# Differential attention: one score tile per map, the turns' bank given up, and low weights times high values only

## The chip, the cores and the metric

The kernel runs on one core of a Trainium2 chip. The metric is the device time of one execution in microseconds; the time of a kernel is the median of its runs. A profiled execution has a time of its own, its span, from the first instruction to the last.

## What is computed

The reference runs two trunk layers of a diffusion generator on 512 latent tokens and 256 context tokens of width 1024. Layer 0 mixes tokens by differential attention, layer 1 by neighbourhood attention; each is followed by a squared-ReLU MLP. What matters here is layer 0's attention, with 8 heads, two maps a head and a head size of 64:

```python
def diff_attend(q, k, v, lam):
    s = jnp.einsum('bqhmd,bkhmd->bhmqk', q, k).astype(jnp.float32) * ATTN_SCALE
    p = jax.nn.softmax(s, axis=-1)
    w = (p[:, :, 0] - lam * p[:, :, 1]).astype(v.dtype)
    return jnp.einsum('bhqk,bkhe->bqhe', w, v)
```

Queries and keys are RMS-normed per map and, on latent tokens, rotated. Context queries see the 256 context keys, latent queries all 768 keys. The output of each head is RMS-normed over its 128 values and goes through a projection.

## The kernel before

**Numbers in two parts.** A matmul operand is kept as a high part (the value rounded to the format that TensorE takes, `F32R`) and a low part (the rest). A product is made of several matmuls: high times high, high times low, low times high.

**Stages.** The kernel goes through five PSUM phases: the first head's projections, the first attention (`psA`), the first MLP, the second attention, the second MLP. PSUM has eight banks per partition of 512 float32 each. `PS_ATTN0` (L55) says how the first attention uses them: `C=1` (one bank for the turned queries and keys), `B=2` (two banks for all other transposes and the weighted sums), `A=2` (projections), `S=1` (one score tile of 1536 columns, three banks, for both maps). A tile of PSUM is given out by `pst` (L106); a new tile of a tag waits until one of its buffers has been read by all its readers.

**One head.** `head0` (L464) has six steps; each works on tiles of 128 tokens, 0 and 1 context, 2 to 5 latent:

- Q, `project` (L493): the projections of a tile, in two halves a and b of twelve matmuls (`qkv_matmul`, L411, the matmuls of L416) into an A tile. After b come norm, rotation and the split of the values into parts (`tile_`, L471).
- U, `turn` (L501): four transposes (L507) put queries and keys of two tiles into one C tile. ACT and DVE then take it out in parts, `q_split` (L435, lines 441 and 442) and `k_split` (L448, lines 452 to 458): copies of the high part on ACT, subtractions for the low part on DVE, in turn, twice, once for each map. U0, U2 and U4 are the three turns of a head.
- S, `scores` (L515): for each map the matmuls of L525 (eight for a latent tile in all, 256 or 512 columns), then maximum (L530, DVE), Exp with sum (L531, ACT), and the difference of the two maps (L537, DVE). In the one score tile the second map begins at column 768, in the middle of the second bank.
- T, `turned` (L541): the weights are transposed (L549), three blocks to a B tile, so a latent tile takes two B tiles in a row and a context tile one; ACT copies the high part (L551), DVE makes the low part (L552).
- V, `weigh` (L554): weights times values into a B tile. Twelve matmuls for a latent tile (four for a context tile), each 256 columns: the value tile holds high and low part side by side, so high weights meet both, and low weights meet both. The two halves are added on the way out (L563 on ACT, L564 on DVE).
- O, `output` (L572): one transpose (L577) into a B tile, copied out by L578.

**Order.** In the first attention PE's, SP's and GpSimd's instructions run in an order written by hand: `START0` for the first heads, then `CYCLE0` five times, then `END0`. A word is a step and a tile, a prime is one head earlier. `run` (L1058) walks through them. DVE's and ACT's order is chosen by the scheduler of the language. The cycle:

```python
CYCLE0 = """w0 w1 Q0a O2'' n1' S1' O3'' V4'' V5'' c0 w2 U4' Q0b c1 w3 Q1a T0' T1' Q1b c2 O4'' S2' V0' Q2a O5'' Q2b
S3' T2' U0 Q3a V1' c3 O0' Q3b S4' T3' Q4a Q4b V2' O1' m0 S5' T4' U2 n0 Q5a V3' Q5b m1 S0 T5'"""
```

The small letters are weight loads (w), their splits (c) and the matmuls that work out modulation vectors (m, n; they hold an A tile in between). `END0` also holds the output projection (P, X, x).

**Behind the attention.** `project.end` (L796) finishes the output projection and norms each pair of tiles; `modulated` (L320) transposes the normed tiles with tag `S`, six pieces of 256 columns to a tile, and ACT and DVE take the pieces out (L337 to L340).

Of the kernel before, what the change touches and what calls it, by code (L numbers as in the profile page):

```python
# [18 lines left out]
P = 128  # L19
D = 1024  # L20
# [3 lines left out]
T = NCTX + NLAT  # L24
# [27 lines left out]
T3' V2' X6 P4b V3' P5a P5b"""  # L52

PS_HEAD0 = dict(A=2, Q2=1, Q0=1, Q1=1, Q3=1, Q4=1, Q5=1)
PS_ATTN0 = dict(C=1, B=2, A=2, S=1)  # L55
PS_MLP0 = dict(D0=1, D1=1, A=2, B=2)
PS_ATTN1 = dict(A=3, S=3, B=2)
PS_MLP1 = dict(A=2, B=2, D1=1, D0=1)
# [5 lines left out]
class Block:  # L64
# [255 lines left out]
    def modulated(self, xns, tiles, l, norm, hT, tag):  # L320

        nc = self.nc
        s = 1 if tiles[0] < 2 else 0
        n = P * len(tiles)
        cols = slice(P * tiles[0], P * tiles[0] + n)
        per = {'S': 6, 'D': 4, 'S1': 2, 'B1': 2}[tag]
        bank = None
        for kt in range(KT):
            if kt % per == 0:
                bank = self.pst(tag[0], (P, 256 * per))  # L330
                for k in range(kt, min(kt + per, KT)):
                    for j, xn in enumerate(xns):
                        o = 256 * (k - kt) + P * j
                        nc.tensor.transpose(bank[:, o:o + P], xn[:, P * k:P * k + P], self.ident)
            ps = bank[:, 256 * (kt % per):]
            f = self.sbt('Y', [P, n])
            nc.scalar.activation(f, ps[:, :n], AF.Identity, bias=self.mB[:, l, norm, kt, s:s + 1],  # L337
                                 scale=self.mA[:, l, norm, kt, s:s + 1])
            nc.vector.tensor_copy(hT[kt][:, 0, cols], f)
            nc.vector.tensor_sub(hT[kt][:, 1, cols], f, hT[kt][:, 0, cols].bitcast(F32))  # L340
# [123 lines left out]
    def head0(self, h, w=None, hT=None, accs=None, split=None):  # L464
# [3 lines left out]
        nc = self.nc  # L468
# [30 lines left out]
                tile_(i, acc.pop(i))  # L499

        def turn(i):  # L501
            ps = self.pst('C')
            for j in range(2):
                y = ys.pop(i + j)
                for c in range(2):
                    o = 256 * c + P * j
                    nc.tensor.transpose(ps[:, o:o + P], y[:, c].rearrange("p m d -> p (m d)"), self.ident)  # L507
            if i == 0:
                here["qk"] = [self.sbt('Q', [P, 2, T], F32R) for _ in range(3)]
            q, kh, kl = here["qk"]  # L510
            cols = slice(P * i, P * i + 256)
            self.q_split(ps[:, 0:256], q, cols)
            self.k_split(ps[:, 256:512], kh, kl, cols, i == 4)

        def scores(i):  # L515
            q, kh, kl = here["qk"]
            nk = NCTX if i < 2 else T
            e = self.sbt('E', [P, 2, T])
            sm = self.sbt('SA', [P, 2])
            ps = self.pst('S', (P, 1536))  # L520
            for m in range(2):
                s = ps[:, T * m:T * m + nk]
                for c0, c1 in ((0, 256),) if i < 2 else ((0, 512), (512, 768)) if m == 0 else ((0, 256), (256, 768)):
                    for p, k in enumerate((kh, kl)):
                        nc.tensor.matmul(s[:, c0:c1], q[:, m, P * i:P * i + P], k[:, m, c0:c1],  # L525
                                         start=p == 0, stop=p == 1)
            for m in range(2):
                s = ps[:, T * m:T * m + nk]
                mx = self.sbt('SA', [P, 1])
                nc.vector.tensor_reduce(mx, s, op=ALU.max, axis=AX, negate=True)  # L530
                nc.scalar.activation(e[:, m, :nk], s, AF.Exp, bias=mx[:, 0:1], accum_out=sm[:, m:m + 1])  # L531

            r = self.sbt('SA', [P, 2])
            nc.vector.reciprocal(r, sm)
            cf = self.sbt('SA', [P, 1])
            nc.vector.tensor_scalar(cf, r[:, 1:2], sm[:, 0:1], self.neglam[:, 0:1], op0=ALU.mult, op1=ALU.mult)
            nc.vector.scalar_tensor_tensor(e[:, 0, :nk], e[:, 1, :nk], cf[:, 0:1], e[:, 0, :nk],  # L537
                                           op0=ALU.mult, op1=ALU.add)
            soft[i] = e, r
# [14 lines left out]
        def weigh(i):  # L554
            nkt = 2 if i < 2 else NT
            wT, r, v = wTs.pop(i), soft.pop(i)[1], here["v"]
            po = self.pst('B')
            jobs = [(x, kt) for c in range(0, nkt, 3) for x in range(2) for kt in range(c, min(c + 3, nkt))]
            for x, kt in jobs:
                nc.tensor.matmul(po[:, :256], wT[:, x, P * kt:P * kt + P], v[:, kt].rearrange("p a d -> p (a d)"),  # L560
                                 start=(x, kt) == jobs[0], stop=(x, kt) == jobs[-1])
            o = self.sbt('O', [P, P])
            nc.scalar.activation(o, po[:, 128:256], AF.Copy, scale=r[:, 0:1])  # L563
            nc.vector.scalar_tensor_tensor(o, po[:, 0:128], r[:, 0:1], o, op0=ALU.mult, op1=ALU.add)  # L564
            so = self.sbt('SO', [P, 1])
            on = ons[i] = self.sbt('O', [P, P])
            nc.scalar.activation(on, o, AF.Square, scale=1.0 / math.sqrt(128.0), accum_out=so[:, 0:1])
            ro = self.rstd(so, 1, 'SO')
            nc.vector.scalar_tensor_tensor(on, o, ro[:, 0:1], self.one[:, 0:1].to_broadcast([P, P]),
                                           op0=ALU.mult, op1=ALU.mult)  # L570
# [14 lines left out]
        for i in accs or ():  # L585
            tile_(i, accs[i])
        steps = dict(Q=project, U=turn, S=scores, T=turned, V=weigh, O=output)
        return lambda kind, i: steps[kind](i)

# [483 lines left out]
def hybrid_block(tc, a, out):  # L1073
    nc = tc.nc
    with ExitStack() as ctx, ExitStack() as st:
# [18 lines left out]
        w = {1: b.load_qkv(a["wqa"], 1, "WB")}  # L1094
        with b.psum_phase("psA", **PS_ATTN0):
            proj, raws = {}, {}
# [175 lines left out]
```

## Time and profile before

| | |
|---|---|
| median of 3 runs | 1869.21 us (1867.21 to 1869.78) |
| span of the profiled execution | 1866.8 us |
| PE busy | 1743.6 us, 93% |
| DVE busy | 1263.1 us, 68% |
| GpSimd (POOL) busy | 1032.8 us, 55% |
| ACT busy | 947.1 us, 51% |

The first attention lies between about 66 and 510 us of the span. PE's matmuls overlap in the profile: a matmul of 256 columns shows about 0.28 us, though one starts every 0.12 us, so a row of several gives the time from the first start to the last end. A row of the timeline has start, length, engine, line, operation, tiles and count, and in brackets the idle time of the engine just before it and what ended it. `PB` is a PSUM tile of tag B, and so on.

### The profile page before, as it was taken

The page shows a single profiled execution, that of the slowest core. Times are in us where ns is not written, and L with a number is a line of the kernel's source. Part 1 is how long each engine was busy: PE and PEld are TensorE (multiplying, and loading weights), DVE is VectorE, ACT ScalarE, POOL GpSimd, SP SyncE. Part 2 cuts the span into 40 slices and gives each one's busy share as a digit, 9 for nine tenths or more (in the row PEclk, how much of TensorE's full clock was granted, in tenths as well). Part 3 has the DMA queues.
Part 4 walks back from the last instruction along what each step waited for, and adds up shares of the span by engine and source line. Part 5 has one row for each costly group of instructions (what it writes and reads, how often), then busy time and mean ns, then how long its engine had stood idle before and what let it go on. Part 6 is the DMA issues. An engine that isn't in the chain of part 4 may idle for free.

```text
span 1866.8 us, 27773 instructions
## 1 busy us (share of the span) xinstructions
PE 1743.6 (93%) x10046; PEld 1524.4 (82%) x10046; DVE 1263.1 (68%) x2333; ACT 947.1 (51%) x2002; POOL 1032.8 (55%) x1008
## 2 busy tenths in 40 slices
PE   6989999996999999999999998999998989999988
PEld 5878888984789888888887987988997778888767
DVE  4587777786665465465466775777777567777686
ACT  4476667765344333333233345777776344544432
POOL 3755666653334555555555733344355557788774
PEclk9999999998999999999999998999999989999989
DMA  8122222224535656645642321122112433344432
GB/s 334 43 86 80 89 88 70 68 85 150 179 113 166 183 164 161 192 163 164 195 154 96 119 97 60 57 83 74 63 63 91 141 113 125 124 130 152 137 116 77
DMA packets 88554, 225.97 MB, mean 121 GB/s; under 512 B 9248, under 2 KB 24544, under 8 KB 82272
## 3 DMA queue, kind: packets, MB, share of 16 engines
q1 hardware_dynamic: 78928, 211.19, 35.1%
q10 hardware_dynamic: 9488, 13.00, 1.9%
q8 instruction: 79, 1.29, 0.3%
q14 instruction: 59, 0.48, 0.1%
HBM read 205.91 MB, written 18.25 MB: 120 GB/s over the span
## 4 chain that ended last, share of the span: by engine, by line
PE 62%; DVE 11%; POOL 8%; ACT 7%; issue 6%; DMA 5%; ACTq 0%; POOLq 0%; SPq 0%; DVEq 0%
PE PD L853 18%; PE PA L416 15%; POOL W L152 6%; PE PB L913 5%; PE PA L913 5%; PE PA L761 4%; DMA R<-in_w_dram 3%; PE PA L991 2%; PE PB L560 2%; PE PA L263 2%; PE PS L525 2%; ACT W L146 2%; PE PQ L406 1%; PE PS L664 1%; PE PB L710 1%
## 5 line engine op out<-in xcount | busy, mean ns | idle before, releaser
L152 POOL TENSOR_TENSOR W<-R,W 128x512 fp32r<-128x512 f32 x270 | 402.6, 1518 | 165.1 <-ACT W L146 162.5
L853 PE MATMUL PD<-Q,W 128*128 128x384 f32 (+2 forms) x1992 | 390.2, 346 | 11.0 <-DVE Q L340 5.6
L853 PEld LDWEIGHTS PD<-Q,W 128*128 128x128 f32 x1992 | 345.4, 189 | 42.3 <-issue 7.8
L146 ACT ACTIVATE W<-R 128x1024 fp32r<-128x1024 f32 (+1 forms) x165 | 168.0, 1022 | 201.2 <-DMA R<-in_w_dram 43.5
L152 POOL TENSOR_TENSOR W<-N,W 128x512 fp32r<-128x512 f32 x98 | 138.8, 1437 | 142.5 <-ACT W L146 138.3
L913 PE MATMUL PB<-W,H 128*128 128x512 f32 x738 | 191.5, 396 | 6.3 <-DVE Q L921 4.4
L913 PE MATMUL PA<-W,H 128*128 128x512 f32 x732 | 190.5, 396 | 6.7 <-DVE H L921 4.4
L416 PE MATMUL PA<-W,Q 128*128 128x384 f32 (+1 forms) x1008 | 175.8, 326 | 1.0 <-ACT H L454 1.0
L913 PEld LDWEIGHTS PB<-W,H 128*128 128x128 f32 x738 | 139.0, 190 | 39.0 <-DVE Q L921 5.3
L913 PEld LDWEIGHTS PA<-W,H 128*128 128x128 f32 x732 | 137.2, 190 | 39.6 <-DVE H L921 5.7
L302 POOL TENSOR_TENSOR SQ<-SQ,half 128x4 f32<-128x4 f32 (+1 forms) x96 | 93.6, 976 | 124.5 <-DVE SQ L429 123.6
L416 PEld LDWEIGHTS PA<-W,Q 128*128 128x128 f32 x1008 | 159.9, 192 | 1.2 <-ACT H L454 1.2
L146 ACT ACTIVATE W<-N 128x1024 fp32r<-128x1024 f32 x49 | 51.8, 1058 | 147.8 <-PE PA L913 66.4
L416 PE MATMUL PA<-WB,H 128*128 128x384 f32 x576 | 110.0, 343 | 0.8 <-DVE Q L477 0.8
L761 PE MATMUL PA<-W,H 128*128 128x512 f32 x384 | 97.7, 405 | 6.0 <-ACT H L752 4.4
L416 PEld LDWEIGHTS PA<-WB,H 128*128 128x128 f32 x576 | 100.2, 191 | 1.7 <-DVE Q L477 1.1
L853 PE MATMUL PD<-H,W 128*128 128x512 f32 (+1 forms) x408 | 94.7, 382 | 0.0
L871 DVE SCALAR_TENSOR_TENSOR H<-N,H 128x512 fp32r<-128x512 f32 (+1 forms) x57 | 68.2, 1201 | 38.7 <-ACT H L870 38.4
L761 PEld LDWEIGHTS PA<-W,H 128*128 128x128 f32 x384 | 72.3, 194 | 24.2 <-ACT H L752 4.8
L531 ACT ACTIVATE E<-PS,SA 128x768 f32<-128x768 f32 (+1 forms) x96 | 72.9, 759 | 36.6 <-DVE SA L530 33.0
L530 DVE TENSOR_REDUCE SA<-PS 128x1 f32<-128x768 f32 (+1 forms) x96 | 74.5, 776 | 24.5 <-ACT E L531 12.0
L676 POOL TENSOR_SCALAR E<-E,SA 128x256 f32<-128x256 f32 x64 | 59.3, 938 | 52.3 <-DVE SA L673 51.6
(258 smaller groups left out, 3568.4 us busy)
## 6 DMA issues: line engine op xcount, KB each, us to landing
R<-in_w_dram SPq DMA_DIRECT2D x121, 512.0 KB
M<-in_wmod_dram SPq DMA_DIRECT2D x48, 1024.0 KB
N<-in_w_dram SPq DMA_DIRECT2D x49, 512.0 KB
R<-in_wqa_dram SPq DMA_DIRECT2D x32, 384.0 KB
R<-in_wqb_dram SPq DMA_DIRECT2D x32, 384.0 KB
Y<-in_rpb_dram SPq DMA_DIRECT2D x48, 128.0 KB
bias<-Y SPq DMA_DIRECT2D x48, 128.0 KB
X<-bias SPq DMA_DIRECT2D x8, 768.0 KB
```

The costliest lines, as they stand in the source:

```text
L146: high = nc.scalar.activation(w[:, 0, :n], raw, AF.Copy)
L152: low = (eng or nc.gpsimd).tensor_sub(w[:, 1, o:e], raw[:, o:e], w[:, 0, o:e].bitcast(F32))
L263: nc.tensor.matmul(ps[32 * q:32 * q + 32, 0:256], self.silu[:, kt, :], raws[kt], start=kt < 4, stop=kt >= 4)
L302: nc.gpsimd.tensor_tensor(r, ss, self.half[:, :n], op=ALU.pow)
L416: nc.tensor.matmul(acc[:, :n], hT[kt][:, x, P * i:P * i + P], w[kt // 2][:, y, o:o + n], start=(kt == 0 and p == 0), stop=(kt == KT - 1 an ...
L530: nc.vector.tensor_reduce(mx, s, op=ALU.max, axis=AX, negate=True)
L531: nc.scalar.activation(e[:, m, :nk], s, AF.Exp, bias=mx[:, 0:1], accum_out=sm[:, m:m + 1])
L676: nc.gpsimd.tensor_scalar_mul(e[:, 1, o:o + 256], e[:, 1, o:o + 256], r[:, 1:2])
L761: nc.tensor.matmul(ps, oHL[h][:, x, c:c + P], w[h // 2][:, y, 512 * (h % 2):512 * (h % 2) + 512], start=(first and h == hs[0] and p == 0), ...
L853: nc.tensor.matmul(ps[:, at:at + b1 - b0], w[kt // 4][:, x, o:o + P], hT[kt][:, y, b0:b1], start=(kt == 0 and p == 0), stop=(kt == KT - 1 ...
L871: nc.vector.scalar_tensor_tensor(u[:, 1], src, 1.0, u[:, 0].bitcast(F32), op0=ALU.mult, op1=ALU.subtract)
L913: nc.tensor.matmul(ps, u[:, x, f, P * i:P * i + P], w[:, y, 512 * f:512 * f + 512], start=(f == 0 and p == 0), stop=(f == 1 and p == 2))
```

## The change

The first attention's PSUM is divided anew: the score tile is two banks wide, there are two of them in turn, and each map has one of its own. The matmuls, maximum and Exp of a map now follow each other in the program. The bank of tag C goes, and a turn takes a B tile. The modulation that runs at the end of the phase puts four pieces into a tile instead of six. In the weighted sum low weights meet only the high part of the values, 128 columns instead of 256: the product of low weights and low values is left out.

```diff
-PS_ATTN0 = dict(C=1, B=2, A=2, S=1)
+PS_ATTN0 = dict(B=2, A=2, S=2)
...
-        per = {'S': 6, 'D': 4, 'S1': 2, 'B1': 2}[tag]
+        per = {'S': 4, 'D': 4, 'S1': 2, 'B1': 2}[tag]
...
         def turn(i):
-            ps = self.pst('C')
+            ps = self.pst('B')
...
             sm = self.sbt('SA', [P, 2])
-            ps = self.pst('S', (P, 1536))
             for m in range(2):
-                s = ps[:, T * m:T * m + nk]
-                for c0, c1 in ((0, 256),) if i < 2 else ((0, 512), (512, 768)) if m == 0 else ((0, 256), (256, 768)):
+                s = self.pst('S', (P, 1024))[:, :nk]
+                for c0, c1 in ((0, 256),) if i < 2 else ((0, 512), (512, 768)):
                     for p, k in enumerate((kh, kl)):
                         nc.tensor.matmul(s[:, c0:c1], q[:, m, P * i:P * i + P], k[:, m, c0:c1],
                                          start=p == 0, stop=p == 1)
-            for m in range(2):
-                s = ps[:, T * m:T * m + nk]
                 mx = self.sbt('SA', [P, 1])
                 nc.vector.tensor_reduce(mx, s, op=ALU.max, axis=AX, negate=True)
                 nc.scalar.activation(e[:, m, :nk], s, AF.Exp, bias=mx[:, 0:1], accum_out=sm[:, m:m + 1])
...
             for x, kt in jobs:
-                nc.tensor.matmul(po[:, :256], wT[:, x, P * kt:P * kt + P], v[:, kt].rearrange("p a d -> p (a d)"),
+                n = (256, P)[x]
+                nc.tensor.matmul(po[:, :n], wT[:, x, P * kt:P * kt + P], v[:, kt].rearrange("p a d -> p (a d)")[:, :n],
                                  start=(x, kt) == jobs[0], stop=(x, kt) == jobs[-1])
```

## The prediction

> **What bounds the kernel now.** I read the page first, then the busy time by stretch, then PE's waits in the first attention, then PE's, DVE's and ACT's timelines of one head, since the diff touches nothing behind that stage. The page gives the profiled execution's own time, 2.4 us under the 1869.2 us median of the runs; I work on the span and add 2.4 us at the end.
>
> ```profile
> span 1866.8 us, 27773 instructions
> ```
>
> The next view gives PE's busy time in three stretches of the first attention: its start, one whole cycle (one head's work for PE, 49.1 us), and its end, where the output projection mixes in.
>
> ```profile
> 85.00:179.00 94.00, 85.75 (x556) 74.25 (x555) 74.33 (x174) 64.48 (x186) 57.92 (x79) 0.98 0.21 75
> 277.30:326.40 49.10, 47.52 (x326) 43.99 (x326) 38.65 (x93) 34.69 (x101) 30.52 (x42) 1.00 0.24 83
> 422.00:470.00 48.00, 30.93 (x146) 22.84 (x145) 28.20 (x59) 24.06 (x63) 17.60 (x21) 0.79 0.46 158
> ```
>
> In a cycle PE is busy 47.52 of 49.10 us: PE sets its length, and at most 1.6 us of waiting can be won there. PE's order is written by hand, so a wait in front of one matmul delays everything behind it. The start has 8.2 us of idle PE and the end 17.1 us. The table of waits says what PE stood for; of it the one score tile (released by the Exp, L531) makes the largest row:
>
> ```profile
> PE PS L525 <- ACT E L531: 10.2, 10, 3.2
> PE PS L525 <- ACT Q L454: 8.2, 8, 2.3
> ```
>
> So the double score tile can win about 10.2 us over 85 to 510 us, and any new wait in a cycle is paid in full, five times (the loop runs five such cycles).
>
> **The change, part by part.**
>
> *Turns in B.* A turn's tile is read by four to five ACT and as many DVE steps, one after the other, and lives long; so far it had a bank to itself. Now it takes one of the two B banks, and while it lives all other B tiles (transposed weights T, weighted sums V, output transposes O) share the other. I take it that a tile gets the bank that comes free first: in the kernel before as compiled, B tiles sometimes get the same bank twice running. Five places in a cycle, each from the rows of one.
>
> T1 behind T0, with turn 4 alive (U4 at 280.84, T0 and T1 are the four transposes at 285.45):
>
> ```profile
> 280.84 0.60 PE L507 MATMUL PC<-ident,Y 128*128 128x128 f32 x4
> 281.20 4.42 PE L416 MATMUL PA<-WB,H 128*128 128x384 f32 x24
> 285.45 0.60 PE L549 MATMUL PB<-ident,E 128*128 128x128 f32 x4
> ```
>
> ```profile
> 286.28 0.43 DVE L552 TENSOR_TENSOR X<-PB,X 128x256 fp32r<-128x256 f32 x1 [0.33 <-ACT X L551]
> ```
>
> ```profile
> 289.80 0.38 ACT L454 ACTIVATE Q<-PC 64x256 fp32r<-64x256 f32 x1
> ```
>
> Turn 4 is read until 290.18 at least, T0's bank until 286.71. T1 now starts near 285.67 (two transposes after 285.45), so it would wait 1.04 us; the matmuls of Q1b, O4 and S2 are queued behind it.
>
> U0 behind T2, and O0 behind V1:
>
> ```profile
> 297.58 0.85 PE L549 MATMUL PB<-ident,E 128*128 128x128 f32 x6 [0.20 <-DVE E L537]
> 298.26 0.60 PE L507 MATMUL PC<-ident,Y 128*128 128x128 f32 x4
> 298.62 2.33 PE L416 MATMUL PA<-WB,H 128*128 128x384 f32 x12
> 300.79 0.64 PE L560 MATMUL PB<-Q,X 128*128 128x256 f32 x4
> 301.26 0.27 PE L577 MATMUL PB<-ident,O 128*128 128x128 f32 x1
> ```
>
> ```profile
> 298.74 1.01 DVE L552 TENSOR_TENSOR X<-PB,X 128x384 fp32r<-128x384 f32 x2
> ```
>
> ```profile
> 302.02 0.35 DVE L564 SCALAR_TENSOR_TENSOR O<-PB,SA,O 128x128 f32<-128x128 f32 x1
> ```
>
> T2 fills both banks; its first is free after the first of the two L552, near 299.25, and U0 wants one at 298.26: 0.99 us. V1 takes T2's second bank; O0 at 301.26 has V1's (free at 302.37) or U0's (later): 1.11 us. Behind them stand Q3a and Q3b, with ACT's copies of their results.
>
> T3's second tile, with U0 alive:
>
> ```profile
> 304.88 0.84 PE L549 MATMUL PB<-ident,E 128*128 128x128 f32 x6
> ```
>
> ```profile
> 306.98 1.02 DVE L552 TENSOR_TENSOR X<-PB,X 128x384 fp32r<-128x384 f32 x2
> ```
>
> ```profile
> 307.71 0.38 ACT L454 ACTIVATE Q<-PC 64x256 fp32r<-64x256 f32 x1
> ```
>
> It would start near 305.2; the first half's bank is free near 307.5, U0's at 308.1. Both come late because ACT and DVE have other work queued. As the rows stand that is 2.3 us; nothing at all if U0's reads close up; I take 1.4 us, near the other four. Behind it stand Q4a and Q4b.
>
> U2 behind T4:
>
> ```profile
> 313.88 0.81 PE L549 MATMUL PB<-ident,E 128*128 128x128 f32 x6
> 314.53 0.60 PE L507 MATMUL PC<-ident,Y 128*128 128x128 f32 x4
> ```
>
> ```profile
> 314.95 1.01 DVE L552 TENSOR_TENSOR X<-PB,X 128x384 fp32r<-128x384 f32 x2
> ```
>
> Free near 315.46: 0.93 us, with n0 and Q5a behind it. The five come to 1.04 + 0.99 + 1.11 + 1.4 + 0.93 = 5.5 us a cycle (4.1 to 6.4).
>
> *Two score tiles.* Three waits in a cycle can go:
>
> ```profile
> 277.28 0.75 PE L525 MATMUL PS<-Q,Q 128*128 128x256 f32 x4 [0.38 <-ACT E L531]
> ```
>
> ```profile
> 290.23 0.96 PE L525 MATMUL PS<-Q,Q 128*128 128x512 f32 x2 [1.04 <-ACT Q L454]
> ```
>
> S1's 0.38 us goes. S2's 1.04 us is a wait for turn 4's last keys, which the change doesn't hasten; but PE now comes there later by T1's wait, so some 0.9 us of it is swallowed. T2's 0.20 us (row above) goes as the two maps' maximum and Exp no longer share a bank. That is 1.5 us. The second map's keys are now cut at 512 columns instead of 256: as many columns and matmuls, no cost.
>
> *Low weights times high values.* 28 matmuls a head go from 256 to 128 moving columns:
>
> ```profile
> 260.58 1.60 PE L560 MATMUL PB<-Q,X 128*128 128x256 f32 x12
> ```
>
> The second attention (L710) has matmuls of 128 columns: durations, then the two in order of time with their weight loads.
>
> ```profile
> L710 PEld LDWEIGHTS PB<-N,VM x2: 192/192/192, 1173.4 to 1173.5; 128*128 128x128 f32 x2
> L710 PE MATMUL PB<-N,VM x2: 273/274/275, 1173.4 to 1173.5; 128*128 128x128 f32 x2
> ```
>
> ```profile
> 1173.36 0.30 PEld L710 LDWEIGHTS PB<-N,VM 128*128 128x128 f32 x2
> ```
>
> ```profile
> 1173.42 0.39 PE L710 MATMUL PB<-N,VM 128*128 128x128 f32 x2
> ```
>
> Twelve of 256 columns take 1.60 us, the last 0.28 of it: 120 ns from one to the next. Two of 128 columns take 0.39 us, the last 0.275 of it: 115 ns; their weight loads are 0.30 − 0.192 = 108 ns apart. The load becomes the limit, not the columns. With the load as the limit both kinds of a group gain, 5 to 12 ns on each of 448 matmuls, 2.2 to 5.4 us; I take 4 us, 0.5 us a head.
>
> [...]
>
> *Modulation in banks of four.* Eight transposes per tile instead of twelve, two tiles in turn. PE's waits name none for these banks, so nothing is to be won. ACT empties six pieces in one go while PE runs projection matmuls:
>
> ```profile
> 530.62 2.84 ACT L337 ACTIVATE Y<-PS,mB,mA 128x256 f32<-128x256 f32 x6 [2.66 <-PE PS L334]
> ```
>
> ```profile
> 530.34 1.86 PE L761 MATMUL PA<-W,H 128*128 128x512 f32 x7
> ```
>
> I cost it at nothing; with that cover gone, 2.84 us a call at most, three calls. No DMA, and nothing on SP's or POOL's queues, is moved.
>
> *Start and end of the stage.*
>
> ```profile
> 81.70 0.66 PE L507 MATMUL PC<-ident,Y 128*128 128x128 f32 x4 [3.36 <-ACT Q L454]
> ```
>
> ```profile
> 425.72 0.74 PE L525 MATMUL PS<-Q,Q 128*128 128x256 f32 x4 [3.18 <-ACT E L531]
> ```
>
> ```profile
> 444.02 2.93 PE L525 MATMUL PS<-Q,Q 128*128 128x512 f32 x8 [3.23 <-ACT E L531]
> ```
>
> At the start a turn waits 3.36 us for the single C bank; with two banks that goes. The start holds five turns, 5/3 of a cycle's new waits: 9.1 us; against it 3.36, the start's part of the score-tile row (10.2 less 6.4 at the end less five times 0.38: 1.9) and 0.7 of weights: +3.1 us (−4 to +9, since idle DVE and ACT may swallow more). At the end 3.18 and 3.23 go, less about 1 us for the second map's tile and 1 us for turn 4 behind V4, and 0.6 of weights: −5 us (−8 to 0).
>
> *Sum.* A cycle: 5.5 − 1.5 − 0.5 = +3.5, five of them +17.5; start +3.1; end −5. Together +15.6 us: span 1882.4, time 1885 us.
>
> **Rivals.**
>
> *Faster.* The scheduler that orders ACT and DVE empties turns early, because PE's waits leave them room: T1 and T3 then find a free bank, and only U0, O0 and U2 still wait, 3.0 us, against 2.0 us won: +1.0 a cycle. With start and end at −4 and −8 that is 5 − 12 = −7 us: 1862 us. It decides from where the new waits of a cycle fall under 2.0 + 12/5 = 4.4 us. For it: ACT is busy 34.7 and DVE 38.7 of 49.1 us, so there is room. Against it: three of the five waits are a bare ACT step and DVE step behind the transposes, and can't shrink.
>
> *Much slower: banks in strict turn.* T1 then waits for turn 4 (290.18 − 285.67 = 4.5 us) and O0 for U0 (308.09 − 301.26 = 6.8 us): 9.2 us more a cycle, +46, 1931 us. Same bank twice running speaks against it.
>
> *Low products at half price.* Waits as forecast, with low matmuls that cost their columns alone: at the 60 ns that a pair shows here,
>
> ```profile
> 1173.24 0.34 PE L710 MATMUL PB<-N,H 128*128 128x128 f32 x2
> ```
>
> (0.34 less 0.28 for the last, as for 256 columns), 224 × 60 ns = 13.4 us instead of 4: +6 us, 1875 us, still slower. The pair's next two are 115 ns apart, so 60 doesn't last. [...]
>
> *No difference.* New waits and wins cancel: the forecast with 4.4 us a cycle on each side, 1869 us.
>
> **How the numbers follow.** The forecast has 0.63, the low products at half price 0.04, strict turn 0.06; faster 0.15; no difference 0.12. What can be told from no change is about 0.2%, 3.7 us. Slower is 0.63 + 0.04 + 0.06 = 0.73. The range: low, 1864 us, lies between the faster rival and no difference and leaves out half of the first; high, 1906 us, is a cycle at 6.4 − 1.5 − 0.2 = +4.7 (24), start +9, end 0, modulation 4 on top. The strict turn lies outside. The forecast's own range is 1867 (a cycle at 4.1 − 1.5 − 0.7 = +1.9, start −4, end −8) to 1906.
>
> **What would show it.** In the profile after: cycles of about 52.6 us instead of 49.1; PE idle in front of L549, L577 and L507 for L552, L564 or L551, about 1 us each; L525 no longer waiting for L531; weight matmuls of a group about 110 ns apart; the end of the stage shorter by 5 us; everything behind 560 us as before, shifted. Wrong, if the cycles are 49 us or less, or if PE's wait for L454 stands in front of L549.

## The result and the profile after

The changed kernel takes 1892.57 us (median of 4 runs, 1887.84 to 1898.45), the kernel before, beside it, 1869.49 us (4 runs, 1867.21 to 1872.5): the ratio is 1.0116, with a 95% interval of 1.0098 to 1.0134. It is slower by 18 to 25 us. The profiled execution of the changed kernel is the fastest of its four, 1887.84 us with a span of 1886.0 us; the other three had a granted clock of 0.976 to 0.978 instead of its 0.985. So what follows explains the 19.2 us between the two spans, and some 4 us of the medians lie outside it.

The span and the busy time come first, from the page of the kernel after.

```profile
span 1886.0 us, 27781 instructions
...
PE 1739.6 (92%) x10046; PEld 1520.8 (81%) x10046; DVE 1269.4 (67%) x2333; ACT 948.2 (50%) x2002; POOL 1043.4 (55%) x1008
```

PE is busy 4.0 us less than before (1743.6) and the span is 19.2 us longer: its busy time went down, and 23 us of waiting came. Where it came is seen by stretch. The next rows hold the start of the attention, one cycle and the end, in the columns of the rows shown of before (stretch, length, busy time of PE, PEld, DVE, ACT and POOL with their instructions, granted clock, DMA share, GB/s).

```profile
85.00:187.00 102.00, 85.94 (x563) 75.18 (x562) 78.45 (x184) 67.88 (x196) 60.62 (x81) 0.98 0.21 73
289.76:342.20 52.44, 47.18 (x330) 43.99 (x328) 39.08 (x94) 34.84 (x101) 31.89 (x43) 1.00 0.23 79
449.00:490.00 41.00, 27.97 (x147) 19.88 (x146) 27.26 (x57) 23.68 (x62) 16.18 (x19) 0.88 0.55 196
```

A cycle takes 52.44 us where it took 49.10, with PE at 47.18 and not 47.52 us: 5.26 us of waiting instead of 1.58. PE's waits in that cycle are four, and they are all there is:

```profile
301.75 0.44 PE L546 MATMUL PB<-ident,E 128*128 128x128 f32 x2 [0.93 <-DVE X L549]
...
314.40 0.63 PE L507 MATMUL PB<-ident,Y 128*128 128x128 f32 x4 [1.80 <-DVE X L549]
...
318.97 0.33 PE L575 MATMUL PB<-ident,O 128*128 128x128 f32 x1 [1.42 <-DVE O L562]
...
333.45 0.63 PE L507 MATMUL PB<-ident,Y 128*128 128x128 f32 x4 [1.11 <-DVE X L549]
```

They stand before T1, U0, O0 and U2 (L546, L575, L549 and L562 are before's L549, L577, L552 and L564; L507 is the turn in both), and each waits for the copy out of a B bank. 0.93 + 1.80 + 1.42 + 1.11 = 5.26. The table of PE's waits over 85 to 530 us says the same of the whole phase:

```profile
PE PB L507 <- DVE X L549: 15.4, 11, 1.8
PE PB L546 <- DVE X L549: 10.2, 7, 3.2
PE PB L575 <- DVE O L562: 7.1, 5, 1.5
...
PE PS L524 <- ACT E L528: 2.4, 4, 1.2
```

The first three rows, 32.7 us, did not exist before. The last is what is left of the waits for the score tile, 10.2 us before.

Both programs have 10046 matmuls, so the start of the same-numbered matmul in both traces gives PE's delay at any point:

| place (time in the kernel before) | delay of the kernel after |
|---|---|
| 54.6 us, ahead of the attention | +3.8 |
| 76.1, first matmuls of the attention | +4.5 |
| 179.4, about the end of its start | +7.8 |
| 251.3, 300.8, 350.2 (328 matmuls apart, one cycle) | +13.0, +16.2, +19.4 |
| 415.8, end of the cycles | +27.0 |
| 497.0, in the projection behind the attention | +19.6 |
| 559.6, in the modulation | +18.6 |
| 604.5, in the MLP | +22.3 |
| 1862.0, last matmul | +19.2 |

The first 3.8 us arise ahead of anything that the change touches. The profiles of the other kernels of this study have +0.5 to +4.6 us there, with no order in it, so 4 us is how far one profiled execution may be off before the change has done anything.

### The profile page after: what moved, and what is told of

Same layout as the page of the kernel before. It is cut to its first block, busy times and chain, and to the rows that moved or that the text cites. A ratio compares the mean times of both kernels' runs of the same rounds, so it can differ in the third digit from the quotient of the medians.

```text
span 1886.0 us, 27781 instructions
## 1 busy us (share of the span) xinstructions
PE 1739.6 (92%) x10046; PEld 1520.8 (81%) x10046; DVE 1269.4 (67%) x2333; ACT 948.2 (50%) x2002; POOL 1043.4 (55%) x1008
## 3 DMA queue, kind: packets, MB, share of 16 engines
q8 instruction: 79, 1.29, 0.3%
## 4 chain that ended last, share of the span: by engine, by line
PE 68%; DVE 11%; ACT 6%; POOL 6%; issue 4%; DMA 4%; ACTq 0%; POOLq 0%; DVEq 0%
PE PD L851 20%; PE PA L416 15%; PE PB L911 6%; PE PA L911 6%; POOL W L152 5%; PE PA L759 4%; PE PA L263 2%; PE PB L558 2%; PE PA L989 2%; PE PS L524 2%; DMA R<-in_w_dram 2%; ACT W L146 2%; PE PQ L406 1%; PE PS L662 1%; DVE SA L527 1%
## 5 line engine op out<-in xcount | busy, mean ns | idle before, releaser
L851 PE MATMUL PD<-Q,W 128*128 128x384 f32 (+2 forms) x1992 | 391.4, 347 | 11.6 <-DVE Q L340 7.1
L416 PE MATMUL PA<-W,Q 128*128 128x384 f32 (+1 forms) x1008 | 175.9, 327 | 1.0 <-ACT H L454 1.0
L416 PEld LDWEIGHTS PA<-W,Q 128*128 128x128 f32 x1008 | 160.1, 192 | 1.2 <-ACT H L454 1.2
L416 PE MATMUL PA<-WB,H 128*128 128x384 f32 x576 | 108.5, 340 | 1.8 <-DVE Q L477 1.8
L416 PEld LDWEIGHTS PA<-WB,H 128*128 128x128 f32 x576 | 98.7, 188 | 2.6 <-issue 2.5
L851 PEld LDWEIGHTS PD<-H,W 128*128 128x128 f32 x408 | 74.6, 191 | 14.9
L416 PE MATMUL PA<-WA,H 128*128 128x384 f32 x432 | 83.9, 345 | 0.0
```

Of the source, the lines that this page charges most:

```text
L416: nc.tensor.matmul(acc[:, :n], hT[kt][:, x, P * i:P * i + P], w[kt // 2][:, y, o:o + n], start=(kt == 0 and p == 0), stop=(kt == KT - 1 an ...
L851: nc.tensor.matmul(ps[:, at:at + b1 - b0], w[kt // 4][:, x, o:o + P], hT[kt][:, y, b0:b1], start=(kt == 0 and p == 0), stop=(kt == KT - 1 ...
```

## The experiments

All are compared with the kernel before on the same chip. Three things are asked: which part of the change costs what, whether the waits are a matter of PE's order, and whether the rest of the loss can be won back. A third B bank was not run, though the first experiment leaves a bank spare for it; so what the number of banks alone is worth stays open.

**The turn in a B bank alone.** The kernel before, without its C bank; the score tile stays one.

```diff
-PS_ATTN0 = dict(C=1, B=2, A=2, S=1)
+PS_ATTN0 = dict(B=2, A=2, S=1)
...
-            ps = self.pst('C')
+            ps = self.pst('B')
```

> The kernel before with one part of the change: the turns take a B tile and the C bank is given up (seven banks used, one spare); scores, weighted sums and modulation as before. Theory (waits for B banks): PE stands in front of T1, U0, O0 and U2 as in the changed kernel, 5.3 us a cycle, against which only 0.9 us of S2's wait is won: a cycle of about 53.5 us, five of them +22; start about +5 (the new waits less the 3.4 us for the C bank), end about +1: 1869 + 28 = 1897 us, a little slower than the changed kernel, because the wins of the two score tiles are missing. Rival (the score tiles, or the order that ACT and DVE get from them, make the loss): within 5 us of the kernel before.

Measured: 1907.77 us (1905.35 to 1909.07), ratio 1.0197 (1.0184 to 1.0210), +37 us. PE's waits over 85 to 530 us:

```profile
PE PB L549 <- DVE X L552: 12.6, 8, 4.2
PE PS L525 <- ACT E L531: 9.1, 5, 3.9
PE PB L577 <- DVE O L564: 9.0, 5, 1.8
PE PB L507 <- DVE X L552: 6.3, 7, 1.0
PE PB L507 <- POOL SQ L302: 5.6, 4, 1.4
```

The waits for B banks are there without any other part of the change, so the theory stands and the rival falls. The loss is 9 us larger than expected, and the start has most of that: by matmuls of the same number, 12 us arise in the start (5 expected), 23 in the five cycles (22), and the end wins nothing (1 lost). The last row is U0's wait, which the profile puts down to a step on POOL. The row for L531 explains none of the excess, as the kernel before waits 10.2 us there. Part of it is the clock. The next rows hold the same 586 matmuls of the start, in the kernel before, in the changed one and in this one:

```profile
76.10:179.40 103.30, 91.69 (x586) 79.87 (x586) 81.86 (x194) 67.87 (x197) 63.98 (x86) 0.97 0.20 70
80.56:187.16 106.60, 89.76 (x586) 78.73 (x586) 82.99 (x195) 68.79 (x198) 63.63 (x86) 0.98 0.20 71
77.27:192.48 115.21, 96.39 (x586) 82.80 (x586) 84.35 (x194) 68.94 (x198) 63.41 (x86) 0.93 0.19 65
```

PE is idle for 11.6, 16.8 and 18.8 us, but it is also busy 4.7 us longer here than in the kernel before, with the same matmuls at a clock of 0.93. The lower clock comes with this kernel: its mean over the whole was 0.973 to 0.977 in all four executions, and 0.977 to 0.985 in those of the kernel before beside it.

Against this kernel the changed one is 15 us shorter in the medians. By matmuls of the same number it is 8.6 us shorter in the start, 4 in the cycles and 8 at the end; the spans differ by about the same, 20.2 us (1906.2 and 1886.0), as 3.3 us that it loses ahead of the attention and 3 us that it wins behind it cancel. Of the 8.6 us only 2.0 are waiting, the rest is busy time, at a clock of 0.98 instead of 0.93. So this profile doesn't tell how much of the start the two score tiles win.

**Low weights times high values alone.** The kernel before, with only that line of the change.

```diff
+                n = (256, P)[x]
-                nc.tensor.matmul(po[:, :256], wT[:, x, ...], v[:, kt].rearrange("p a d -> p (a d)"),
+                nc.tensor.matmul(po[:, :n], wT[:, x, ...], v[:, kt].rearrange("p a d -> p (a d)")[:, :n],
```

> The kernel before with one part of the change: low weights meet high values only (128 columns; the product of low weights and low values is left out). Theory (the weight load sets the pace): a group of twelve matmuls takes 1.49 us instead of 1.60 us, 56 matmuls a head, about 4 us in all: 1865 us (1864 to 1867). Rival (a matmul costs its columns): 12 to 13 us, 1857 us. If the weighted sums are hidden behind other waits: no change.

Measured: 1869.86 us (1867.57 to 1874.51), ratio 1.0001 (0.9992 to 1.0010): no difference, against both numbers. Two rows of PE's timeline, a group of weighted sums and scores 2:

```profile
263.53 1.49 PE L561 MATMUL PB<-Q,X 128*128 128x256 f32 x12
...
292.97 0.96 PE L525 MATMUL PS<-Q,Q 128*128 128x512 f32 x2 [1.04 <-ACT Q L454]
```

The group of twelve does take 1.49 us and not 1.60, as forecast, and from one start to the next the weighted sums of a cycle take 0.5 us less. But the three middle cycles are each only 0.25 us shorter than before. The waits don't take the difference: scores 2 still wait 1.04 us for turn 4, and the other two waits of a cycle are as long as before, to 0.02 us. It goes into the matmuls behind the weighted sums, most of which take 0.02 to 0.05 us more each time (twelve of L416 behind a group, for one, 2.30 us at 321.49, where the kernel before has 2.25 at 318.94). The delays are larger by 1.5 us at the end of the start and by 2.0 us in the last cycle, more than the middle ones win; in the last cycle stands a stretch of 3.41 us at half the clock, and the start was not traced.

The same was asked the other way round, in the changed kernel, with the 256 columns put back:

> The changed kernel with the product of low weights and low values computed again (256 columns instead of 128 for low weights). Theory (with the many waits for the banks of B the shorter groups are swallowed by the next wait, as in the kernel before): within 1.5 us of the changed kernel, 1891 to 1894 us. Rival (the 4 us that the prediction put down for it are real here): 1896 us or more.

Measured: 1891.31 us (1889.76 to 1896.92), ratio 1.0117 (1.0100 to 1.0133), that of the changed kernel within its interval. The four waits of a cycle are 0.93, 1.80, 1.28 and 1.11 us, the third shorter by 0.14 as PE comes later, and the middle cycles are 0.15 to 0.2 us longer, not 0.5. So a wait for a copy takes 0.14 us of what is saved, the matmuls behind the weighted sums about as much again, and 0.2 us a head, 1.6 in all, is less than this pair of medians can show.

**The modulation in fours alone.** The kernel before with `per = {'S': 4, ...}`.

> The kernel before with modulation in tiles of four pieces instead of six at the end of the first attention (one such tile at a time, in the place of the score tile). The profile after lost some 3 us on PE in this place (558 to 569 us of before), in front of the first matmuls of the MLP. Theory (the change of the pieces costs what the prediction put at nothing): +1 to +3 us, 1870 to 1872 us. Rival (that loss is a shift between two profiles): 1869 us, no change.

Measured: 1874.39 us (1871.06 to 1877.49), ratio 1.0019 (1.0009 to 1.0028), +3.6 us. The prediction put nothing there. PE's waits of 525 to 600 us, first in the kernel before, then in this one:

```profile
PE PD L853 <- DVE Q L339: 1.0, 1, 1.0
PE PS L334 <- DVE N L317: 0.9, 2, 0.7
PE PD L853 <- ACT X L863: 0.3, 1, 0.3
```

```profile
PE PD L853 <- DVE Q L340: 3.0, 3, 1.7
PE PD L853 <- DVE Q L339: 1.1, 1, 1.1
PE PD L853 <- ACT X L863: 0.7, 1, 0.7
```

The MLP's first matmuls wait for the modulated tiles (L339 and L340 write them): 4.1 us against 1.0. So the cover that the prediction named, projection matmuls, ends before the last modulation does. Behind it stands the MLP, which needs its result.

The same part was undone in the changed kernel: the two score tiles are given back once the last scores are read, and one of three banks takes their place, so that six pieces fit again.

```diff
+            b.ps_s.close()
+            b.psum['S'] = b.ps_s.enter_context(tc.tile_pool(name="psAE", bufs=1, space=PSUM, reuse_waits="tile"))
+            b.pbufs['S'] = 1
             proj["end"]()
...
-        per = {'S': 4, 'D': 4, 'S1': 2, 'B1': 2}[tag]
+        per = {'S': 6, 'D': 4, 'S1': 2, 'B1': 2}[tag]
```

> The changed kernel, in which the two score tiles are given back once the last scores are read, and a tile of three banks takes their place, so that the modulation behind the attention has six pieces to a tile again. Theory (the modulation in fours costs some 3 to 4 us there, as it did in the kernel before): 2 to 4 us shorter than the changed kernel, about 1888 to 1890 us, with PE's matmuls up to 550 us where they are in the changed kernel. Rival (in the changed kernel the wait comes from the shifted work in front of it, not from the pieces): within 1 us of the changed kernel.

Measured: 1893.01 us (1884.64 to 1896.11), ratio 1.0110 (1.0092 to 1.0128). At its place the loss is gone: between the 497 and the 605 us of before, PE's delay stays at 22.7 us, where it goes from 19.6 to 22.3 in the changed kernel. In the time of the whole nothing of it is seen; the intervals, 3.4 us to each side, would hide 3 us. Undecided.

**The order spread.** If the waits are a matter of the order, other work of PE's put between the users of the B banks takes them away. The changed kernel, with T0 moved ahead of half a projection and U0, O0, T3 and U2 moved behind one:

```diff
-... c1 w3 Q1a T0' T1' Q1b c2 ... S3' T2' U0 Q3a V1' c3 O0' Q3b S4' T3' Q4a Q4b ... T4' U2 n0 Q5a V3' ...
+... c1 w3 T0' Q1a T1' Q1b c2 ... S3' T2' Q3a U0 V1' c3 Q3b O0' S4' Q4a T3' Q4b ... T4' n0 Q5a U2 V3' ...
```

> The changed kernel with the same words of the cycle in another order, so that half a projection (2.1 us of PE) stands between two users of B wherever a turn holds the other bank: T0 Q1a T1, T2 Q3a U0 V1 Q3b O0, S4 Q4a T3, T4 n0 Q5a U2. Theory: the waits in front of T1, U0, O0 and U2 (5.3 us of a cycle of 52.4 us) go nearly all; up to 1.5 us comes back at T3's and T5's second tiles, as U0 and U2 begin 2 us later, and S2's wait for turn 4 returns with about 1 us: cycles of 48.5 to 50.5 us, 1870 to 1882 us in all. Rival (the loss lies in the shared load of ACT and DVE, not in where PE stands): cycles stay over 51.5 us, 1888 us or more.

Measured: 1884.0 us (1880.23 to 1890.55), ratio 1.0075 (1.0058 to 1.0092): 8 us of the loss are won back. That lies between the two: the theory had 1870 to 1882 us, the rival 1888 or more. A cycle takes 51.15 us. The numbers in brackets are its waits:

```profile
299.79 0.84 PE L524 MATMUL PS<-Q,Q 128*128 128x256 f32 x2 [0.83 <-ACT Q L454]
...
318.61 0.55 PE L546 MATMUL PB<-ident,E 128*128 128x128 f32 x3 [1.61 <-ACT Q L454]
...
335.17 0.55 PE L546 MATMUL PB<-ident,E 128*128 128x128 f32 x3 [0.75 <-ACT Q L454]
```

The four are gone, 5.26 us, and three others have come, 3.19 us. (The cycle is shorter by 1.29 us and not by the difference, as PE's busy time rose from 47.18 to 47.81 us; why was not traced.) Scores 2 wait for turn 4 again, and the second tiles of T3 and T5 now wait for the banks of U0 and U2, which are turned later and read for as long as before. A wait of that kind is what the prediction had put at T3's second tile.

Two further orders go after these. The second moves T3 and T5 on by a step (T3 behind Q4b and m0 behind it, T5 into the next cycle behind Q0a):

> The changed kernel with every turn moved at least one PE slot away from the neighbours that share its bank pair, and T3 and T5 moved one slot on (T3 from right behind Q4a to behind Q4b, T5 from the end of one head group to the start of the next). Theory (the loss is the waits for the two banks that turns and transposes share, and it is a matter of the order): the waits of PE for the copies out of those banks fall from about 5.3 us a cycle in the changed kernel and about 2.5 to 3 in the first spread order to under 1, a cycle takes 48.8 to 49.8 us and not 52.4, and the whole 1868 to 1876 us. Rival (the pair of banks is short whatever the order, and each wait taken away turns up at the next user): cycles stay over 51 us and the whole at 1882 or more.

Measured: 1882.15 us (1879.69 to 1884.72), ratio 1.0069 (1.0056 to 1.0081): the rival. A cycle takes 51.48 us, and each tile that was moved has a new neighbour:

```profile
287.77 0.33 PE L575 MATMUL PB<-ident,O 128*128 128x128 f32 x1 [1.45 <-DVE X L549]
...
301.14 0.85 PE L524 MATMUL PS<-Q,Q 128*128 128x256 f32 x2 [0.82 <-ACT Q L454]
...
323.10 1.59 PE L558 MATMUL PB<-Q,X 128*128 128x256 f32 x12 [1.34 <-DVE X L549]
```

O2 waits for T5's copies, V2 for T3's. The third order puts work without a B tile in there: n1 and scores 1 between T5 and O2, V0 ahead of scores 2, and m0 ahead of T3 with Q4b behind it.

> The second spread order with three moves more in the cycle: scores 1 and n1 between T5 and O2, V0 ahead of S2 instead of O4, and m0 between Q4a and T3, with Q4b behind T3. Theory (the remaining waits of that order, 1.45 before O2, 1.34 before V2, 0.83 before S2, are a matter of the order): a cycle of 49 to 50 us instead of 51.1, the whole 1872 to 1878 us. Rival (each wait turns up at the next user of the two banks): within 2.5 us of the second spread order, 1880 us or more.

Measured: 1879.35 us (1877.39 to 1881.25), ratio 1.0046 (1.0033 to 1.0058). The cycle, its stretch and three of its waits:

```profile
286.65:336.78 50.13, 47.92 (x329) 43.63 (x328) 39.73 (x94) 34.68 (x102) 32.51 (x42) 1.00 0.23 83
```

```profile
287.95 0.33 PE L575 MATMUL PB<-ident,O 128*128 128x128 f32 x1 [0.58 <-DVE X L549]
...
318.42 0.55 PE L546 MATMUL PB<-ident,E 128*128 128x128 f32 x3 [0.24 <-ACT Q L454]
...
321.95 1.59 PE L558 MATMUL PB<-Q,X 128*128 128x256 f32 x12 [0.90 <-DVE X L549]
```

PE works 47.92 of 50.13 us, so 2.2 us of waiting are left of 5.26. The cycle came out just above its expected 49 to 50, the time 1.35 us above the expected 1878. So most of the loss in a cycle is a matter of the order, but not all of it in any order tried: 49.1 us was not reached.

That order with the modulation in sixes as well:

> The third spread order together with the modulation in sixes at the end of the phase. Theory (the two gains are in different places and add): 2 to 4 us shorter than the third spread order alone, 1868 to 1876 us, about as fast as the kernel before. Rival (what is gained at the modulation is lost behind it): within 1 us of the third spread order alone.

Measured: 1879.33 us (1877.73 to 1884.03), ratio 1.0046 (1.0033 to 1.0059): the rival, no difference. In the modulation PE's delay stays at 7.8 us where it rose from 6.9 to 8.5 without it, so the local gain is there once more, 1.6 us, and once more the time doesn't show it.

**The start.** The second spread order with the rotating tiles of the attention put on other banks of the first head's phase, because the changed kernel's map had a wait that the prediction did not see:

```diff
-PS_HEAD0 = dict(A=2, Q2=1, Q0=1, Q1=1, Q3=1, Q4=1, Q5=1)
+PS_HEAD0 = dict(A=2, Q0=1, Q1=1, Q2=1, Q3=1, Q4=1, Q5=1)
```

> The kernel of the second spread order, and beside it the start's four Q tiles and the rotating pair put on other banks, so that the rotating pair begins on the banks of the first two Q tiles instead of the third and first. Theory (the changed bank map made PE wait 1.8 us at 69.6 us of the changed kernel for the copy of a later Q tile): that wait goes and the whole is 1 to 2.5 us shorter than the kernel of the second spread order, 1866 to 1874 us. Rival (the copies behind it end at the same time, so the wait turns up at the next tile): within 0.7 us of the kernel of the second spread order.

Measured: 1886.46 us (1883.17 to 1886.89), ratio 1.0087 (1.0073 to 1.0101): 4 us slower than the second order, and neither theory. The wait at that place fell from 1.78 to 0.79 us; the profile can't be read for more, as the granted clock in its start was low (in the last section). Whether the clock or the map makes the 4 us stays open.

Last, the start and the end written anew by the rule that worked in the cycle, with the third order and the modulation in sixes. All words of the three orders stay; the start's middle, for instance, becomes

```
T0'' Q4b' S2'' V0'' n0 T1'' S3'' V1'' Q5a' T2'' m2 Q5b' U0' O0'' S4'' w0 w1 Q0a n2 T3'' S5'' O1'' V2''
Q0b c0 w2 U2' S0' Q1a O2'' T4'' Q1b V3'' c1 w3 U4' m3 V4'' O3'' S1' T0' c2 Q2a n3 O4'' V0' T5'' Q2b V5'' S2' T1'
```

> The third spread order in the cycle and the modulation in sixes, and the start and the end of the phase spread by the same rule: no use of the two banks right behind a pair of transposed tiles, no turn less than some 8 us ahead of a pair. Theory (the start's 10 us of waits for the two banks are a matter of the order as well): the start ends 3 to 7 us earlier, the end 1 us, the whole 1871 to 1877 us, no faster than the kernel before. Rival (the start has too little other work on PE, so that the waits only move): 1878 us or more.

Measured: 1883.37 us (1882.08 to 1888.37), ratio 1.0072 (1.0058 to 1.0086): the rival, and worse than without it. The profiled execution took 1888.37 us, 5 us more than the median. The waits for T's tiles in the start have shrunk, from 8.6 us in the second order (which has the same start as the third) to 3.5. In their place stands:

```profile
PE PB L576 <- DVE O L568: 8.3, 2, 4.8
```

L576 is the output step (L575 above) and L568 the norm ahead of it: PE came to O before its data were normed. The longer of the two waits is O5's, which stands only S2 and T1 behind its own V; the other, O0's, was not traced. By matmuls of the same number the start ends no earlier than with the third order (+11.1 us at 179 us against +8.9), and the end wins 2 us instead of 7. No order tried is faster than the kernel before.

## Why the prediction was right

It forecast 1885 us (1864 to 1906) and slower with a chance of 0.73; the time is 1892.57 us.

**New waits in a cycle: right in sum, not in each.** Forecast 5.5 us, measured 5.26. T1 (1.04; 0.93) and U2 (0.93; 1.11) came out within 0.2 us. U0 and O0 were larger (0.99 and 1.11; 1.80 and 1.42), and T3's second tile, put at 1.4, does not wait at all. The copies out of T2's tiles show why U0 waits longer:

```profile
312.31 0.49 ACT L548 ACTIVATE X<-PB 128x384 fp32r<-128x384 f32 x1 [0.86 <-PE PB L546]
...
313.70 0.55 DVE L549 TENSOR_TENSOR X<-PB,X 128x384 fp32r<-128x384 f32 x1
```

ACT's copy of the first tile ends at 312.80, but DVE's subtraction starts only at 313.70, as DVE is busy with other things: 1.92 us behind the start of the transposes, where the kernel before had 1.16 (298.74 less 297.58). And by the time PE gets to T3, turn 0 has been read:

```profile
321.05 0.38 ACT L454 ACTIVATE Q<-PB 64x256 fp32r<-64x256 f32 x1
...
322.62 0.82 PE L546 MATMUL PB<-ident,E 128*128 128x128 f32 x6
```

T3 starts 8.2 us behind U0 (314.40), where it was 6.6 us, 1.4 of the 1.6 us being O0's wait; and turn 0 is read for 7.0 us from U0's start, where it was 9.8. The prediction had said that T3 waits for nothing if those reads close up, and put 1.4 us all the same. That is one step that failed: the prediction took each wait from rows of before, as if those in front of it moved nothing. The order spread shows it from the other side: with U0's and O0's waits gone, T3's second tile waits 1.61 us.

**Banks as they come free: right.** Strict turn would have made T1 wait 4.5 us. It waited 0.93.

**Wins in a cycle: right.** The waits of scores 1, scores 2 and T2 are gone. 5.26 − 1.58 of waits less 0.34 of PE's work (47.18 instead of 47.52 us) make +3.34 us, against +3.5 forecast; by the delays, the middle cycles run at +3.25. Over all five it is +19.3 against +17.5; in the last one T1 waits 3.24 us.

**Start: right in sum, partly by luck.** Forecast +3.1 us, measured 7.8 − 4.5 = +3.3. By the rows of the 586 matmuls, PE's idle time grew by 5.2 us, where the forecast had 9.1 − 3.36 − 1.9 = 3.8; and its busy time fell by 1.9 us, where it had 0.7, with the clock at 0.98 instead of 0.97. The turn's wait of 3.36 us is gone, but m0 (L263) waits 2.37 us for an A tile where it waited for nothing; why was not traced. Nor was this wait foreseen, as the rotating A tiles now begin on banks that held later Q tiles:

```profile
69.64 6.49 PE L416 MATMUL PA<-WB,H 128*128 128x384 f32 x36 [1.78 <-DVE Q L477]
```

Before, the same place waited 0.79 us. It stands ahead of the attention's first matmuls, so its 1.0 us is in the +4.5 and not in the +3.3.

**End: right.** Forecast −5 us (−8 to 0), measured 19.6 − 27.0 = −7.4. The two waits of 3.18 and 3.23 us are 0.71 and 1.18 now. The same 352 matmuls, before and after:

```profile
415.80:497.00 81.20, 64.12 (x352) 49.76 (x351) 48.55 (x105) 39.15 (x101) 23.86 (x31) 0.87 0.40 143
442.82:516.59 73.77, 60.74 (x352) 46.40 (x351) 46.63 (x99) 37.77 (x99) 22.14 (x28) 0.93 0.44 158
```

So 4.05 us of the 7.4 are waiting. The other 3.4 are PE's busy time, of which the forecast had 0.6; the clock is 0.93 there instead of 0.87.

**Low weights: right in the group, wrong in the sum.** The row of a group in the kernel after, with 0.28 us for its last matmul, gives (1.49 − 0.28) / 11 = 110 ns from one to the next:

```profile
327.44 1.49 PE L558 MATMUL PB<-Q,X 128*128 128x256 f32 x12
```

That is about the spacing that the forecast took from the weight loads of L710, 108 ns. The twelve loads of this group take 1.52 us, which with 0.19 for the last is 121 ns from one to the next. That the load sets the spacing was the author's estimate and is not shown by itself. Six low matmuls at the 60 ns that a pair showed before would have made the group 1.60 − 6 × 0.06 = 1.24 us, so low products at half price are not what the trace shows. Over the whole PE is busy 4.0 us less, just what was put down, but that proves nothing: with this part alone in the kernel before, it was busy 3.2 us more (1746.8 us). Of the 0.5 us a head, 0.25 was left in a cycle of the kernel before and 0.15 to 0.2 in the changed one, and nothing showed in the time, in either experiment. The failed step is to have summed what a group saves as time won: the matmuls behind it gave part of it back, and in the changed kernel a wait for a copy took another 0.14 us.

**Modulation in fours: wrong.** Put at nothing with 2.84 us a call as the bound; it costs 3.6 us alone in the kernel before, and +2.7 at its place in the changed one (19.6 to 22.3).

Put together, from the attention's first matmuls to the MLP: 3.3 + 19.3 − 7.4 + 2.7 = 17.9 us, where the forecast had 15.6: the modulation adds 2.7 us and the cycles 1.8, and the end takes 2.4 off. The rest of the 7.6 us between the forecast and the median stands elsewhere: 4.5 us arise ahead of those matmuls, 3.1 are won back behind 604.5 us, and some 4 lie between the profiled execution, with its higher clock, and the median. It was not traced.

Which part costs what, against the kernel before: turns in B +37 us, modulation in fours +3.6, low weights nothing that the medians show. If the parts add, the changed kernel's +23 leaves 37 + 3.6 − 23 = some 18 us that the two score tiles win. That is a difference and no run by itself, and as the first experiment shows, part of it is the clock.

## What to carry to other kernels

A bank that looks idle may be what keeps a long-lived tile out of the way of short-lived ones: before it is given up, count for each tile that shares the rest how long it is read, and look in a hand-written order for every pair of users that stand closer than that. Such waits can be moved by the order, but each one moved lands on the next user until work without that resource lies between all of them, so price a new order as a whole. Work saved on an engine is not yet time saved: look at what stands behind it, the next wait and the next work, in both of which part of the 0.5 us a head was lost here.

## What the runs showed of the hardware

The second spread order was run with the old and with the new bank map. PE's waits around 125 to 141 us are the same in both profiles (2.09, 1.16 and 1.27 us; 2.08, 1.16 and 1.26), but not the granted clock. The stretches of 125 to 155 us, the clock third from the right, first with the old map, then with the new:

```profile
125.00:135.00 10.00, 9.68 (x68) 9.65 (x69) 6.83 (x19) 6.78 (x21) 3.99 (x6) 1.00 0.00 0
135.00:145.00 10.00, 7.40 (x57) 5.17 (x56) 7.74 (x20) 7.25 (x23) 4.61 (x6) 1.00 0.26 75
145.00:155.00 10.00, 9.32 (x59) 8.65 (x58) 8.07 (x18) 6.98 (x19) 5.35 (x7) 1.00 0.34 136
```

```profile
125.00:135.00 10.00, 9.18 (x54) 9.15 (x55) 6.24 (x17) 5.90 (x18) 2.42 (x4) 0.83 0.00 0
135.00:145.00 10.00, 7.41 (x48) 5.09 (x47) 6.05 (x16) 6.54 (x18) 6.59 (x8) 0.78 0.18 54
145.00:155.00 10.00, 10.00 (x59) 9.31 (x58) 7.25 (x19) 5.92 (x19) 3.18 (x5) 0.88 0.47 158
```

At a granted clock of 0.78 to 0.88 PE gets through fewer matmuls in the same time, 161 instead of 184 in 30 us; by matmuls of the same number it loses 3.9 us there.

Cut where the clock changes, the profiles show only 1.00 and 0.50. Between 60 and 600 us the kernel before has half the clock for 3.41 us three times, for 6.83 and for 10.24 us once each, the changed kernel for 3.41 us twice and for 10.24 us once: 3.41 us, or two or three times that. First the new map around the wait of 2.08 us, then the old one around that of 2.09:

```profile
123.47:126.88 3.41, 1.32 (x10) 1.09 (x9) 2.79 (x7) 3.33 (x9) 1.06 (x3) 1.00 0.00 0
126.88:130.29 3.41, 3.41 (x15) 3.41 (x13) 1.77 (x4) 0.78 (x4) 0.00 (x0) 0.50 0.00 0
```

```profile
120.56:123.97 3.41, 2.67 (x19) 2.26 (x18) 2.46 (x7) 2.65 (x9) 0.39 (x1) 1.00 0.12 38
123.97:127.38 3.41, 2.06 (x13) 2.07 (x14) 2.81 (x7) 2.64 (x7) 0.94 (x2) 1.00 0.00 0
127.38:130.79 3.41, 3.41 (x27) 3.41 (x26) 2.27 (x6) 2.55 (x8) 0.35 (x1) 1.00 0.00 0
```

With the new map the whole wait falls into one stretch, PE is idle for 2.09 of its 3.41 us, and the next runs at half the clock. With the old map the wait is shared by two stretches, idle for 0.74 and 1.35 us, and the clock stays. Cut into such stretches between 60 and 600 us, the profiles of the kernel before and of the changed one have 303 at full clock. Eight of them are followed by half the clock, and PE was idle for 1.24 to 3.37 us of those; of the other 295 none was idle for more than 1.80 us. In between, both occur: in the changed kernel the stretch at 311.84 us was idle for 1.80 us and the clock stayed, the one at 584.91 us was idle for 1.24 us and half the clock followed. So the wait of 2.08 us was followed by half the clock and that of 2.09 us was not, by where each fell: in the 3.41 us behind them PE got through 15 and through 27 matmuls. By matmuls of the same number these two profiles, with the same waits, differ by the 3.9 us named above.
